# SwiGLU's down projection in seven block products for twelve of 22 hidden tiles

## The chip, the cores and the metric

The kernel runs on one core of one Trainium2 chip. Five engines work side by side, each through its own instructions in order: TensorE (PE, with weight loads shown apart as PEld), VectorE (DVE), ScalarE (ACT), GpSimd (POOL) and SyncE (SP). DMA transfers are issued by SP (plain ones) and by POOL (those that add to their destination). The metric is the device time of one execution in microseconds, as the median of several runs; lower is better.

## The reference

One step of a decoder layer for 512 prompt tokens and 64 sample tokens, 576 columns together: a mixer, a cross attention and a SwiGLU, each with RMS norms. The change lies in the SwiGLU:

```python
u = _rms(x) * g_pre_ffn
f = (jax.nn.silu(u @ w_gate) * (u @ w_up)) @ w_down
x = x + _rms(f) * g_post_ffn
```

The model width is 1024 (8 tiles of 128), the hidden width 2816 (22 tiles of 128). Everything is float32.

## The kernel before

**Products.** Data lie with features on partitions and the 576 tokens in columns. A float32 product is made of three: each operand is split into a high part, rounded to the type float32r by a copy on ACT, and a low part, the difference, by a subtraction on DVE (`split`, lines 191 to 193; for weights `split_w`, 174 to 189). `gemm` (195 to 204) adds high x high, high x low and low x high into one PSUM bank. Weights come by SP into the buffers "raw" (two) or "rawx" (two), their parts go to "whi" and "wlo" (three each).

**Gate and up.** Hidden tiles 0 to 3 are computed in the ordinary way, in a stretch whose order is written out by hand (`plan`, under `manual_schedule`). From tile 4 on, class `Pair` (line 1645) does two hidden tiles at once, first the gate, then the up projection. It takes the weights of two tiles, halves the 1024 inputs into 2 x 512 and the tokens into 2 x 288 (`E`), and computes the 2 x 2 block product with seven block products for eight: sums and differences of weight blocks are formed on DVE (`sums`, `diffs`), split into parts, and each of the seven factors is multiplied by a prepared block of u (`mul`: 4 k-steps x 3 products of 288 columns). The blocks are added in PSUM and between PSUM and SBUF: `early` (factors 0 and 1), `mid` (2, 3, 4) and `late` (5, 6). `late` runs after the next half's `early`. The low part l1 of the first weight tile has the tag "wacc" (two buffers): ACT writes the negative of the rounded value, then a POOL transfer adds the weight itself from DRAM (`low`, line 1659). `done` puts the activation into `gates(j)` (two sets of four tiles, in turn), multiplies by the up half and splits the product into `hh`, `hl`, the operand of the down projection.

**Down.** `down_chunk` runs over the 8 output tiles and two column ranges of 256 and 320 (`HALVES`). For each it adds the products over the hidden tiles of a chunk: chunk 0 over tiles 0 to 7, chunk 1 over 8 to 15, chunk 2 over 16 to 21. The first chunk's results are copied into `f2` (1800), those of the second are added (1804), those of the last are added together with the sums of squares for the last norm (1859, 1903). `hh` and `hl` lie in the slots s0 and s2, `f2` in slot s4.

**Order.** Behind the hand-ordered stretch, which ends with the `mid` of pair 4's up half, a scheduler fixes each engine's order when the kernel is built: it takes the earliest instruction of the program that its own reckoning says is ready. On the chip each engine keeps that order. The program's order there is: pair 6, chunk 0, pairs 8 to 14, chunk 1, pairs 16 to 20, chunk 2, then a hand-ordered end.

Of the kernel before, what the change touches and what calls it, by code (L numbers as in the profile page):

```python
# [11 lines left out]
F32 = mybir.dt.float32  # L12
F32R = mybir.dt.float32r
# [6 lines left out]
P = 128  # L20
T = 576
# [95 lines left out]
def build(nc, tc, ctx, I, O):  # L117
# [1527 lines left out]
    class Pair:  # L1645

        def __init__(s, j, up, hh, hl):
            s.j, s.up, s.hh, s.hl = j, up, hh, hl
# [71 lines left out]
        def done(s, a, i, ps, more=None):  # L1720
# [12 lines left out]
            k = (s.j + a) % 8  # L1733
            split(s.hh[:, k, E[i]], s.hl[:, k, E[i]], g)
# [25 lines left out]
    def pairs(js, hh, hl, last=None):  # L1760

        for j in js:
            for up in range(2):
                if last and j == 4:
                    continue
                with tc.issue_after((pp[1].ev2 if up else pp[0].ev3).ins) if j == 6 else ExitStack():
                    p = Pair(j, up, hh, hl)
# [5 lines left out]
                last = p  # L1773
        return last
# [22 lines left out]

    def ev_first(n_, j, i, ps, m):
# [9 lines left out]
    for n_ in range(2):  # L1808
        at_(14.0 + n_ / 10, lambda n_: pp.append(Pair(4, n_, *H)), n_)
# [192 lines left out]
def pack(inp):  # L2002
# [38 lines left out]
    out["wdown"] = _units(i["w_down"][0], NFFN)  # L2041
# [46 lines left out]
```

## Time and profile before

| | us |
|---|---|
| median of 3 runs | 1123.84 |
| runs | 1121.85 to 1124.16 |
| span of the profiled execution | 1122.0 |

The span runs from the first to the last instruction; what lies around it isn't in it. In the rows that follow, PE, DVE, ACT and POOL are the engines; "ps_g" and "ps_u" are the PSUM banks of a pair's gate and up half, "ps_dn" those of the down projection, "whi" and "wlo" the parts of weights, "wacc" the low part made by an adding transfer, "gt" the gates, "hh" and "hl" the parts of the hidden tiles. A group of instructions shows, after the names and shapes, its count, its busy time and the mean ns of one, and behind the second bar the idle time of the engine just before it with what ended it. In the timeline the columns are start, duration, engine, line and operation. Records of matmuls overlap: their pace is the distance between starts, not their duration. The list of DMA queues gives packets, MB and the share of 16 engines' time. The page gives KB as 1024 bytes: a 128 x 576 float32 tile has 288.

PE's order in the stage, from the timeline: chunk 0 from about 806.7 us, pairs 8 to 14 from 862.5, chunk 1 with the last block products of pair 14 to about 1005, pairs 16 to 20 to 1066, then chunk 2 and the end.

### The profile page before, as it was taken

How to read it: one execution, taken by the hardware profiler on the slowest of the kernel's cores; microseconds unless marked ns; L12 is line 12 of the kernel's file. 1: busy time of each engine (PE TensorE's matmuls, PEld its weight loads, DVE VectorE, ACT ScalarE, POOL GpSimd, SP SyncE). 2: the span in 40 equal slices, each digit the busy share in tenths (PEclk: the TensorE clock that was granted, in tenths of full speed). 3: DMA queues.
4: the chain of work that ended last, by engine and by line, in shares of the span. 5: the costliest groups of instructions: out<-in, count | busy, mean ns of one | idle time of the engine just before them, and what ended most of it. 6: DMA issues, size and time to landing. Idle time of an engine off the chain costs nothing.

```text
span 1122.0 us, 21140 instructions
## 1 busy us (share of the span) xinstructions
PE 1101.1 (98%) x8427; PEld 1051.6 (94%) x8427; DVE 708.8 (63%) x1395; ACT 595.4 (53%) x1076; POOL 219.3 (20%) x305
## 2 busy tenths in 40 slices
PE   9999999999999999999999999999999999999997
PEld 8999889898998999999988889999999999999997
DVE  6796874457786675668654555767623665446655
ACT  6877533355553365656444455635434675236644
POOL 1333544322122121110144301101001110011000
PEclk9999999999999999999999999999999999999999
DMA  6685565535574447863467855643625775257442
GB/s 213 158 164 129 131 175 158 162 86 141 147 203 107 126 145 266 271 241 109 155 236 281 282 181 174 234 145 92 172 82 126 170 162 141 75 126 172 118 140 85
DMA packets 57127, 181.82 MB, mean 162 GB/s; under 512 B 6300, under 2 KB 10524, under 8 KB 56516
## 3 DMA queue, kind: packets, MB, share of 16 engines
q1 hardware_dynamic: 41444, 137.47, 37.9%
q0 software_dynamic: 15296, 42.47, 18.4%
q8 instruction: 66, 1.08, 0.4%
q10 hardware_dynamic: 288, 0.52, 0.1%
q14 instruction: 33, 0.27, 0.1%
HBM read 158.21 MB, written 22.22 MB: 161 GB/s over the span
## 4 chain that ended last, share of the span: by engine, by line
PE 81%; DMA 6%; DVE 4%; issue 4%; ACT 4%; SPq 0%; POOL 0%; DVEq 0%; ACTq 0%; POOLq 0%
PE ps_in L201 5%; PE ps_in L203 5%; PE ps_in L202 5%; PE ps_dn L201 4%; PE ps_dn L203 4%; PE ps_dn L202 4%; PE ps_u L1717 2%; PE ps_u L1716 2%; PE ps_u L1715 2%; PE ps_g L1715 2%; PE ps_o L201 2%; PE ps_g L1716 2%; PE ps_g L1717 2%; PE ps_o L203 2%; PE ps_o L202 2%
## 5 line engine op out<-in xcount | busy, mean ns | idle before, releaser
L181 ACT CAST whi<-raw 128x1024 fp32r<-128x1024 f32 x110 | 114.7, 1045 | 104.9 <-PE ps_dn L202 20.0
L201 PE MATMUL ps_in<-uh,whi 128*128 128x320 f32 (+1 forms) x544 | 165.9, 305 | 0.0
L203 PE MATMUL ps_in<-uh,wlo 128*128 128x320 f32 (+1 forms) x544 | 163.2, 300 | 0.0
L202 PE MATMUL ps_in<-ul,whi 128*128 128x320 f32 (+1 forms) x544 | 162.7, 299 | 0.0
L188 DVE TENSOR_TENSOR wlo<-raw,whi 128x1024 fp32r<-128x1024 f32 (+1 forms) x102 | 102.0, 1000 | 76.0 <-ACT whi L181 75.6
L201 PEld LDWEIGHTS ps_in<-uh,whi 128*128 128x128 f32 x544 | 103.5, 190 | 2.6 <-issue 1.2
L203 PEld LDWEIGHTS ps_in<-uh,wlo 128*128 128x128 f32 x544 | 103.4, 190 | 1.6 <-issue 1.3
L202 PEld LDWEIGHTS ps_in<-ul,whi 128*128 128x128 f32 x544 | 103.5, 190 | 0.7
L201 PE MATMUL ps_dn<-hh,whi 128*128 128x320 f32 (+1 forms) x280 | 82.7, 298 | 0.0
L203 PE MATMUL ps_dn<-hh,wlo 128*128 128x320 f32 (+1 forms) x280 | 81.9, 294 | 0.6 <-DVE wlo L188 0.6
L202 PE MATMUL ps_dn<-hl,whi 128*128 128x320 f32 (+1 forms) x280 | 82.2, 294 | 0.0
L203 PEld LDWEIGHTS ps_dn<-hh,wlo 128*128 128x128 f32 x280 | 52.8, 189 | 0.8 <-DVE wlo L188 0.8
L202 PEld LDWEIGHTS ps_dn<-hl,whi 128*128 128x128 f32 x280 | 52.8, 188 | 0.0
L201 PEld LDWEIGHTS ps_dn<-hh,whi 128*128 128x128 f32 x280 | 52.3, 188 | 0.3 <-ACT hh L192 0.3
L186 POOL DMA_DIRECT2D wlo<-win x32 | 28.3, 885 | 94.5 <-ACT wlo L185 84.1
L1715 PE MATMUL ps_g<-b,whi 128*128 128x288 f32 x144 | 42.6, 296 | 0.8 <-ACT cc L1751 0.6
L1716 PE MATMUL ps_u<-b,whi 128*128 128x288 f32 x144 | 42.5, 295 | 0.0
L1716 PE MATMUL ps_g<-b,whi 128*128 128x288 f32 x144 | 42.5, 295 | 0.0
L1715 PE MATMUL ps_u<-b,whi 128*128 128x288 f32 x144 | 42.5, 295 | 0.0
L201 PE MATMUL ps_o<-mixm_h,whi 128*128 128x256 f32 (+1 forms) x128 | 38.0, 297 | 1.6 <-ACT whi L181 1.6
L201 PE MATMUL ps_xo<-qh,whi 128*128 128x288 f32 x128 | 38.0, 302 | 1.0 <-ACT f_xo L1407 1.0
L201 PE MATMUL ps_xq<-u2h,whi 128*128 128x320 f32 (+1 forms) x128 | 38.2, 303 | 0.0
(731 smaller groups left out, 3650.3 us busy)
## 6 DMA issues: line engine op xcount, KB each, us to landing
raw<-win SPq DMA_DIRECT2D x35, 512.0 KB, 3.8
raw<-wout SPq DMA_DIRECT2D x17, 512.0 KB, 4.2
kva<-kc SPq DMA_DIRECT2D x16, 512.0 KB, 6.5
kva<-vc SPq DMA_DIRECT2D x16, 512.0 KB, 6.3
raw<-wdown SPq DMA_DIRECT2D x16, 512.0 KB, 3.5
raw<-wxq SPq DMA_DIRECT2D x13, 512.0 KB, 3.7
raw<-wgate SPq DMA_DIRECT2D x13, 512.0 KB, 3.6
raw<-wup SPq DMA_DIRECT2D x13, 512.0 KB, 4.8
```

The source lines that it names most:

```text
L181: A.copy(hi[:, :n], raw[:, :n])
L186: G.dma_start(lo[:, a:b], src[:, a:b], accum_op=ALU.add)
L188: e.tensor_tensor(lo[:, a:b], raw[:, a:b], hi[:, a:b].bitcast(F32), op=ALU.subtract)
L201: mm(ps, wh, ah, start=i == 0, stop=False)
L202: mm(ps, wh, al, start=False, stop=False)
L203: m = mm(ps, wl, ah, start=False, stop=i == len(tiles) - 1)
L1715: mm(ps, wh, b[0][:, k, :], start=start and k == 0, stop=False, skip_group_check=True)
L1716: mm(ps, wh, b[1][:, k, :], start=False, stop=False, skip_group_check=True)
L1717: m = mm(ps, wl, b[0][:, k, :], start=False, stop=k == 3, skip_group_check=True)
```

## The change

Chunk 0 now covers hidden tiles 0 to 3 alone, and comes right behind the hand-ordered stretch. Its results go through two small buffers ("ssq") to a DRAM tile `f2_d`, one transfer on SP for each output tile.

The hidden tiles 4 to 9 and 10 to 15 are taken in two sets. A `Down` makes two output tiles from the three pairs of a set as a 2 x 2 block product with seven block products: 7 x 3 k-steps x 3 products of 288 columns. There are four for each set, alternating between the two groups of PSUM banks. Its weights come as two loads of 128 x 768, are added and subtracted on DVE, and are split into f1, f2, f3 (768 columns, tags "whi" and "wlo") and f4 (384 columns twice, in a buffer of the tag "wacc"). `early`, `mid`, `late` are as in `Pair`; `begin` is the order for the first of a set, around the last pair's `late`. `keep` copies PSUM to the result rows on ACT, `plus` adds PSUM to them on DVE, and `store` sends each row by POOL, with an addition in DRAM, into `f2_d`. Row buffers: the first and third Down use "ssq" tiles, the second and fourth a free half of `gt`.

The operands are formed as the pairs finish: `place`, called by `done`, makes four differences on DVE and seven splits (before, four splits) into a tile of 16 x 288 for each pair, which lies in slot s4, s0 or s2 in turn. So `f2` can't lie in s4 meanwhile: it is loaded from `f2_d` by SP after pair 18, in one transfer of 2304 KB. Pairs 16 to 20 and the last chunk are as before. On the host the rows of `w_down` are put in the order of the sets.

The core of the diff:

```diff
+        def place(s, a, i):
+
+            op, ((g11, g12), (g21, g22)) = s.dst(s.j), gates(s.j)
+
+            def put(m, g):
+                split(op[:, m, :], op[:, 7 + m, :], g)
+
+            if (a, i) != (0, 1):
+                put(a + a * i, (g11, g21, g22)[a + a * i])
+                return
+            minus(g11, g12, g11)
+            minus(g12, g22, g12)
+            minus(g22, g22, g11)
+            put(4, g22)
+            put(3, g11)
+            put(5, g12)
+            minus(g21, g21, g22)
+            put(6, g21)
...
+    class Down:
+
+        def __init__(s, c, n_):
+            s.c, s.j = c, 2 * n_
+            s.r1 = wp.tile([P, 1024], F32, name="raw", tag="raw", bufs=2)[:, :768]
+            s.r2 = fp.tile([P, 1024], F32, name="rawx", tag="rawx", bufs=2)[:, :768]
+            for a, r in enumerate((s.r1, s.r2)):
+                S.dma_start(r, I["wdown"][s.j + a, :, 768 * c - 256:768 * c + 512])
+            if n_ % 2:
+                g4 = gates(6 * c + 2)
+                s.st = [[g4[a][i] for i in range(2)] for a in range(2)]
+                s.rows = [gt[:, 4 * ((3 * c + 1) % 2) + 2 * a:4 * ((3 * c + 1) % 2) + 2 * a + 2, :].rearrange("p i t -> p (i t)") for a in range(2)]
+            else:
+                s.rows = [ph.tile([P, 640], F32, name="fst", tag="ssq", bufs=2)[:, :T] for _ in range(2)]
+                s.st = [[r[:, c_] for c_ in E] for r in s.rows]
...
+        def prepare(s):
+            s.f1 = s.parts()
+            split(*s.f1, s.r1)
+            sw_ = sw[:, :768]
+            V.tensor_tensor(sw_[:, DB], s.r2[:, DA], s.r2[:, DB], op=ALU.add)
+            minus(sw_[:, DA], sw_[:, DB], s.r1[:, DA])
+            s.f2 = s.parts()
+            split(*s.f2, sw_)
+            minus(s.r2[:, DA], s.r1[:, DA], s.r2[:, DA])
+            minus(s.r1[:, DB], s.r1[:, DB], sw_[:, DA])
+            s.f3 = s.parts()
+            split(*s.f3, s.r2)
+            t_ = fp.tile([P, 1024], F32R, name="wacc", tag="wacc", bufs=2)
+            s.f4 = t_[:, DA], t_[:, DB]
+            split(*s.f4, s.r1[:, DB])
...
+        def mul(s, ps, w, m, ks=(0, 1, 2), start=True, stop=True):
+
+            fh, fl = (s.f1, s.f2, s.f3, s.f4)[w // 2]
+            for k in ks:
+                c = slice((3 * (w % 2) + k) * P, (3 * (w % 2) + k + 1) * P)
+                op = operand(6 * s.c - 2 + 2 * k)
+                bh, bl = op[:, m, :], op[:, 7 + m, :]
+                mm(ps, fh[:, c], bh, start=start and k == 0, stop=False, skip_group_check=True)
+                mm(ps, fh[:, c], bl, start=False, stop=False, skip_group_check=True)
+                mm(ps, fl[:, c], bh, start=False, stop=stop and k == ks[-1], skip_group_check=True)
...
+        def begin(s, last):
+
+            s.x, y, s.z = s.bank(), s.bank(), s.bank()
+            s.mul(s.x, 0, 0)
+            s.keep(0, 0, s.x)
+            s.mul(y, 1, 1, (0, 1), stop=False)
+            last.late()
+            s.mul(s.z, 3, 3, (0, 1), stop=False)
+            s.mul(s.x, 2, 4, (0, 1), False, False)
+            s.mul(y, 1, 1, (2,))
+            s.plus(0, 0, y)
+            s.mul(s.x, 2, 4, (2,), False)
+            s.keep(0, 1, s.x)
+            s.mul(s.z, 3, 3, (2,))
+            s.end()
...
+        def early(s):
+            s.x, y = s.bank(), s.bank()
+            s.mul(s.x, 0, 0)
+            s.keep(0, 0, s.x)
+            s.mul(y, 1, 1)
+            s.plus(0, 0, y)
+
+        def mid(s):
+            s.mul(s.x, 2, 4, start=False)
+            s.keep(0, 1, s.x)
+            s.z = s.bank()
+            s.mul(s.z, 3, 3)
+            s.end()
+
+        def end(s):
+            s.mul(s.x, 4, 5, start=False)
+            s.keep(1, 1, s.x)
+            s.plus(1, 1, s.z)
+
+        def late(s):
+            s.mul(s.x, 5, 6, start=False)
+            s.keep(1, 0, s.x)
+            s.store(1)
+            s.mul(s.z, 6, 2, start=False)
+            s.plus(0, 1, s.z)
+            s.store(0)
+
+        def store(s, a):
+            G.dma_start(f2_d[:, s.j + a, :], s.rows[a], accum_op=ALU.add)
+
+    def down_blocks(c, last):
+
+        for n_ in range(4):
+            d = Down(c, n_)
+            d.prepare()
+            if n_ == 0:
+                d.begin(last)
+            else:
+                d.early()
+                last.late()
+                d.mid()
+            last = d
         return last
...
     def ev_first(n_, j, i, ps, m):
         t0, n = HALVES[i]
-        A.copy(f2[:, j, t0:t0 + n], ps)
-
-    def ev_add(n_, j, i, ps, m):
-        t0, n = HALVES[i]
-        V.tensor_tensor(f2[:, j, t0:t0 + n], f2[:, j, t0:t0 + n], ps, op=ALU.add)
+        if j not in firsts:
+            firsts[j] = ph.tile([P, 640], F32, name="fst", tag="ssq", bufs=2)
+        A.copy(firsts[j][:, t0:t0 + n], ps)
+        if i == 0:
+            S.dma_start(f2_d[:, j, :], firsts[j][:, :T])
...
+    w_of = lambda j: weights(("d", j), I["wdown"][j, :, 0:512], 512, cut=512)
+    down_chunk(0, 4, [(j, i) for j in range(8) for i in (1, 0)], pp[1], w_of, ev_first)
+    last = down_blocks(1, pairs((6, 8), operand))
+    last = down_blocks(2, pairs((10, 12, 14), operand, last))
+    hh, hl = SL0("hh2"), SL(2, "hl2", F32R)
+    last = pairs((16, 18), (hh, hl), last)
     f2 = SL(4, "f_ffn")
-
-    for c, (js, ev) in enumerate((((4, 6), ev_first), ((8, 10, 12, 14), ev_add))):
-        if c:
-            hh, hl = SL0("hh%d" % c), SL(2, "hl%d" % c, F32R)
-        last = pairs(js, hh, hl, None if c else pp[1])
-        w_of = lambda j: weights(("d", j, c), I["wdown"][j, :, 1024 * c:1024 * c + 1024], cut=1024)
-        down_chunk(c, 8, [(j, i) for j in range(8) for i in (1, 0)], last, w_of, ev)
-
-    hh, hl = SL0("hh2"), SL(2, "hl2", F32R)
-    last = pairs((16, 18, 20), hh, hl)
+    S.dma_start(f2, f2_d)
+    last = pairs((20,), (hh, hl), last)
```

More of the change, by code (lines that the diff above doesn't have):

```diff
@@ L1758, in late, with operand, pairs @@
             s.done(0, 1, s.z, s.c2)
-    def pairs(js, hh, hl, last=None):
+    operands = {}
+    def operand(j):
+        if j not in operands:
+            make = ((lambda n, d, w: SL(4, n, d, w)), (lambda n, d, w: big0.tile(list(w), d, name=n, tag="s0", bufs=1)),
+                    (lambda n, d, w: SL(2, n, d, w)))[(j - 4) // 2 % 3]
+            operands[j] = make("hop%d" % j, F32R, (P, 16, 288))
+        return operands[j]
+    def pairs(js, dst, last=None):
         for j in js:
             for up in range(2):
-                if last and j == 4:
-                    continue
                 with tc.issue_after((pp[1].ev2 if up else pp[0].ev3).ins) if j == 6 else ExitStack():
-                    p = Pair(j, up, hh, hl)
+                    p = Pair(j, up, dst)
                     p.prepare()
@@ L1773, in pairs, with parts, bank, keep @@
                 last = p
+        return last
+    f2_d = dr.tile([P, KT, T], F32, name="f2_d")
+    DA, DB = slice(0, 384), slice(384, 768)
+    class Down:
[12 more added lines that the diff above has]
+                s.st = [[r[:, c_] for c_ in E] for r in s.rows]
+        def parts(s):
+            return [wp.tile([P, 1024], F32R, name=k, tag=k, bufs=3)[:, :768] for k in ("whi", "wlo")]
+        def prepare(s):
[13 more added lines that the diff above has]
+            split(*s.f4, s.r1[:, DB])
+        def bank(s):
+            return (MP if s.j % 4 else GP)("ps_dn")[:, :288]
+        def mul(s, ps, w, m, ks=(0, 1, 2), start=True, stop=True):
[7 more added lines that the diff above has]
+                mm(ps, fl[:, c], bh, start=False, stop=stop and k == ks[-1], skip_group_check=True)
+        def keep(s, a, i, ps):
+            A.copy(s.st[a][i], ps)
+        def plus(s, a, i, ps):
+            V.tensor_tensor(s.st[a][i], s.st[a][i], ps, op=ALU.add)
+        def begin(s, last):
[37 more added lines that the diff above has]
+            G.dma_start(f2_d[:, s.j + a, :], s.rows[a], accum_op=ALU.add)
```

17 lines of the change are left out of this document (11 added, 6 removed).

## The prediction

> **What bounds the kernel now.** I read the page's head first, then the windows over the stages that the change touches, then PE's waits, and last the rows that price each added operation.
>
> ```profile
> span 1122.0 us, 21140 instructions
> PE 1101.1 (98%) x8427; PEld 1051.6 (94%) x8427; DVE 708.8 (63%) x1395; ACT 595.4 (53%) x1076; POOL 219.3 (20%) x305
> ...
> PE 81%; DMA 6%; DVE 4%; issue 4%; ACT 4%; SPq 0%; POOL 0%; DVEq 0%; ACTq 0%; POOLq 0%
> ```
>
> PE is busy for 98% of the span and carries 81% of the chain that ended last, so a product taken away is worth its pitch, unless PE then waits. The next view is the windows: columns are the stretch, its length, then busy time (instructions) of PE, its weight loads, DVE, ACT and POOL, the granted clock, the DMA share and GB/s. The first row is the old first down chunk (all products over hidden tiles 0 to 7), the second two halves of a gate/up pair, the third the old second chunk. The last three serve further down.
>
> ```profile
> 806.70:862.50 55.80, 55.80 (x422) 55.80 (x421) 18.25 (x24) 19.17 (x33) 2.55 (x3) 1.00 0.43 109
> 899.90:922.10 22.20, 22.20 (x170) 22.20 (x169) 15.47 (x29) 15.79 (x26) 3.35 (x5) 1.00 0.76 166
> 947.50:1005.00 57.50, 56.89 (x429) 56.69 (x428) 24.86 (x40) 14.51 (x19) 2.55 (x3) 1.00 0.41 106
> 355.00:360.00 5.00, 2.97 (x22) 1.65 (x20) 4.54 (x7) 3.50 (x8) 2.20 (x3) 0.87 0.68 166
> 360.00:364.00 4.00, 4.00 (x26) 4.00 (x27) 2.94 (x9) 1.14 (x3) 0.00 (x0) 0.74 0.52 121
> 792.00:796.00 4.00, 2.70 (x21) 2.46 (x20) 3.67 (x8) 3.50 (x7) 0.85 (x1) 1.00 0.90 197
> ```
>
> PE stands nowhere in the stages of the change but at three places; its waits from 740 us on (line that waits, for whom, total, times, longest):
>
> ```profile
> PE ps_u L1717 <- DMA wacc<-wup: 1.3, 1, 1.3
> ...
> PE ps_g L1715 <- ACT cc L1751: 0.6, 1, 0.6
> PE ps_dn L203 <- DVE wlo L188: 0.6, 1, 0.6
> ```
>
> So the stage is a solid train of products, and the question is only how many leave it and what new holes come in.
>
> **Products removed.** One half of a pair, seven blocks of 4 x 3 = 84 products of 288 columns, repeats at equal distance in the chain of waits, and the chunk's products (256 and 320 columns in turn) can be paced in the timeline:
>
> ```profile
> 909.71 0.27 PE ps_g L1717 x2
> ...
> 931.93 0.27 PE ps_g L1717 x2
> ```
> ```profile
> 837.04 0.31 PE L201 MATMUL ps_dn<-hh,whi 128*128 128x320 f32 x1
> ...
> 849.79 0.31 PE L201 MATMUL ps_dn<-hh,whi 128*128 128x320 f32 x1
> ```
>
> (931.93 - 909.71) / 168 = 132.3 ns for 288 columns; from 837.04 to 849.79 lie two output tiles' turns, 96 products, so 12.75 / 96 = 132.8 ns on average. Before, chunks 0 and 1 take 2 x 8 x 2 x 8 x 3 = 768 products, 102.0 us. After, the first chunk covers four hidden tiles, 8 x 2 x 4 x 3 = 192 products, 25.5 us; a Down has 7 blocks x 3 k-steps x 3 = 63 products, 8.33 us, and eight of them take 504 products, 66.7 us. Removed: 102.0 - 92.2 = **9.8 us**. The last chunk (tiles 16 to 21) and all gate and up products stay.
>
> **Holes of before that go.** The 1.3 us wait was pair 6's up half standing for its adding transfer, right behind the hand-ordered stretch. Now chunk 0, 25.5 us with nothing for that transfer to wait on, lies between; that wait goes. So does the 0.6 us of the old second chunk (ps_dn for wlo), since the chunk is gone. The 0.6 us at L1751, inside a pair, I leave. **-1.9 us.**
>
> **Operands formed per pair, and the blocks' weights.** The rows, with mean ns before the second bar:
>
> ```profile
> L193 DVE TENSOR_TENSOR hl<-gt,hh 128x288 fp32r<-128x288 f32 x29 | 13.1, 456 | 12.9 <-ACT hh L192 12.9
> L192 ACT CAST hh<-gt 128x288 fp32r<-128x288 f32 x29 | 12.1, 425 | 8.9 <-DVE gt L1732 8.9
> L1672 DVE TENSOR_TENSOR sw<-rawx 128x512 f32<-128x512 f32 x13 | 8.9, 688 | 0.1
> L1740 ACT COPY cc<-ps_g 128x288 f32<-128x288 f32 x7 | 2.8, 399 | 2.0 <-PE ps_g L1717 2.0
> L188 DVE TENSOR_TENSOR wlo<-rawx,whi 128x768 fp32r<-128x768 f32 x1 | 0.9, 948 | 0.0
> L181 ACT CAST whi<-rawx 128x768 fp32r<-128x768 f32 x1 | 0.8, 834 | 0.7 <-PE ps_g L1716 0.7
> ```
>
> place() makes seven splits where there were four, and four differences: per pair +3 x 0.425 = 1.3 us of ACT, +7 x 0.456 = 3.2 us of DVE. A pair's 22.2 us then hold 15.5 + 3.2 = 18.7 us of DVE and 17.1 of ACT: under PE's time. A Down costs DVE three lows of 768 columns (2.84), five operations on 384 columns (between 456 and 688 ns, I take 550: 2.75) and three additions from PSUM (1.37), 7.0 us; ACT three casts (2.50), one of 384 (0.5) and four copies (1.6), 4.6 us; both against PE's 8.33. So I cost them at nothing: PE's own products cover them. Without that cover the extra DVE work would be 6 pairs x 3.2 = 19 us (a rival below).
>
> **The start of each block set (begin).** Here the chain is short of cover. The last up half's late ends with block 6; from there the k = 2 operand of block 4 needs addition, product, three differences, cast and low part. The trace has the old chain of addition, product, cast, low part in two engines:
>
> ```profile
> 953.75 0.46 DVE L1730 TENSOR_TENSOR ct<-ps_u,cc 128x288 f32<-128x288 f32 x1 [4.45 <-ACT cc L1751]
> 954.24 0.46 DVE L1732 TENSOR_TENSOR gt<-gt,ct 128x288 f32<-128x288 f32 x1
> ...
> 955.20 0.46 DVE L193 TENSOR_TENSOR hl<-gt,hh 128x288 fp32r<-128x288 f32 x1 [0.50 <-ACT hh L192]
> ```
>
> 953.75 to 955.66 is 1.91 us. Three dependent differences add up to 3 x 0.49 (the step from the first row to the second): 3.4 us. begin puts 6 + 6 + 3 = 15 products there, 1.98 us. The gap is 1.4 us, and DVE may be within a 948 ns low part when the chain starts; I take 1.7 us, twice **+3.4 us**. Bounds: nothing, where other products are pulled forward, and 2 x 2.4 us, a whole low part in front.
>
> **From blocks back to pairs.** A Down's fourth factor f4 takes the tag "wacc" with two buffers, which the next pair's l1 needs for its adding transfer. The third Down's buffer comes free with block 6 in its late, which stands between early and mid of the fourth Down. From there: ACT writes the negative, POOL issues, the transfer adds. Once in the trace that chain was bare, at the 1.3 us wait:
>
> ```profile
> 788.88 1.06 ACT L1664 ACTIVATE wacc<-raw 128x1024 fp32r<-128x1024 f32 x1 [2.05 <-DMA raw<-wup]
> ```
> ```profile
> 790.25 0.86 POOL L1665 DMA_DIRECT2D wacc<-wup  x1 [7.78 <-ACT wacc L1664]
> ```
> ```profile
> DMA to landing us min/median/max: 5.0/5.6/7.8
> ```
>
> From issue to landing lie 5.6 us at the median, so 1.4 + 5.6 = 7.0 us from the buffer's release. PE has the fourth Down's mid, 27 products, and its late, 18, plus the four products of the pair's first two blocks that need no low part: 49 x 132.3 ns = 6.5 us, if late is pulled ahead of the pair's early. That leaves 0.5 us at the median and 2.7 at the slowest landing; I take 1.0, twice **+2.0 us**. The up half's l1 gets the fourth Down's buffer at 6.5 us and has the gate's 56 remaining products, 7.4 us, as cover: nothing. Bounds: 0, and for the pulled order not taken 7.0 - 27 x 0.1323 = 3.5 us, twice 7.0.
>
> **Result rows and adding transfers.** Each Down sends two rows of 288 KB by POOL, added in DRAM; its row buffers are used again two Downs later, so the first copy (ACT, keep) of the third and fourth Down waits for the landing, with ACT's later casts behind it, and block 2 behind the copy (same PSUM bank). No row shows an addition into DRAM; the nearest are the additions into SBUF:
>
> ```profile
> wlo<-wgate POOLq DMA_DIRECT2D x7, 256.0 KB, 4.8
> ```
> ```profile
> q1 hardware_dynamic: 7073, 24.96, 29.5%
> q0 software_dynamic: 4032, 11.01, 24.2%
> ```
>
> After block 6 the addition takes 0.6 us, the transfer about 5 (between 256 KB at 4.8 and 512 KB at 5.6), the copy 0.4: 6.0 us. Cover, from the same moment: the new Down's early (18), the other's block 4 (9) and late (18), and block 3 (9), 54 products, 7.1 us, if all of it is pulled forward; 27 products, 3.6 us, if none beyond the first two is. Stall between 0 and 2.4 us; four places; I take 0.5 each, nearer to the first, as PE's train of pairs shows such interleaving without holes: **+2.0 us** (bounds 0 and 9.6). By the Trainium skill, "DMA: Bandwidth & Descriptors", Anatomy of one DMA, a transfer costs about 2.0 us plus its bytes over 436 GB/s, here 2.7 us by my estimate, and this term would be 0; the same section warns that a write into HBM is confirmed slowest, which speaks against the change. The trace disagrees with the figure: 256 KB took 4.8 us.
>
> Load on the engines of DMA: 8 first rows and the final return add 4.7 MB at q1's rate (24.96 MB in 29.5% of 280 us: 302 GB/s), 15.6 us; the 16 additions 4.7 MB at q0's 162 GB/s, 29 us. Over the 280 us from 800 to 1080 that is 16% more share; the chunk's rows above show 0.41 and the pairs' 0.76. SP's first-row stores stand in its queue behind ACT's copies, but weights are fetched two buffers ahead there. The return of f2 on SP (2304 KB, 7.8 us at that rate) stands ahead of pair 20's weights and is itself needed only in the last chunk. Cost: nothing, hidden by pairs 18 and 20; without that cover 7.8 us once.
>
> **Sum.** -9.8 - 1.9 + 3.4 + 2.0 + 2.0 = **-4.3 us**. The profiled execution's span, 1122.0, becomes 1117.7. The median of the runs is 1123.84, 1.84 us above that span; so I forecast 1119.5 us.
>
> **Rivals.**
>
> *All holes filled.* The order written by the scheduler pulls later products forward wherever one waits, as it does between the halves of pairs, where PE shows no hole in 22.20 us. Then only -9.8 - 1.9 and at most 1 us of begin stay: 1113.1. Against: in begin the next Down's first factor needs a cast buffer that the first Down still holds, so little can be pulled.
>
> *Nothing gained.* At the two returns to pairs the order is kept as written, 3.5 us each, and begin takes its upper bound, 4.8: -9.8 - 1.9 + 4.8 + 7.0 + 2.0 = +2.1, so 1125.9 at worst and 1123.4 with one of the two returns. For it: the wait at 790 shows that a landing later than reckoned in the order costs PE directly.
>
> *Slower: the row buffers.* If an addition into DRAM lands after the slowest 7.8 us seen, instead of about 5, the keep comes at 0.6 + 7.8 + 0.4 = 8.8 us, against 3.6 us of sure cover: 5.2 us at four places, 21 us in place of 2, so 1138; with all of the 7.1 us, 1.7 us each, and the total stays at 1124. It decides from where a place costs (9.8 + 1.9 - 3.4 - 2.0) / 4 = 1.6 us. A long hole costs more: after PE's 2.0 us of idleness in 355 to 360 the granted clock fell to 0.87 and 0.74, 0.13 x 5 + 0.26 x 4 = 1.7 us lost, while the 1.3 us hole in 792 to 796 left it at 1.00. With that, four holes of 3 us would give 1119.5 - 2 + 4 x 4.7 = 1136. By the Trainium skill, "TensorE: Matmul & The Clock Gate", What's actually happening, the gate closes only after an idle window of about 3.4 us; here it fell after 2.0.
>
> *DVE becomes the bound.* 18.7 of 22.2 us speaks against; if the additions could not overlap, 19 us more, 1138.5.
>
> **How the numbers follow.** Forecast 0.42 (1116 to 1122), all filled 0.22, nothing gained 0.19, row buffers 0.13, DVE 0.04. A difference of 0.2%, 2.2 us, is about what the measurement of this kernel can tell from none: faster is below 1121.6. Faster: 0.22 + 0.9 x 0.42 = 0.60. Same: 0.04 of the forecast and 0.16 of "nothing gained", 0.20; slower the rest, 0.20. The range runs from all filled, 1112.5, to 1130, which takes in returns and begin at their upper bounds with two of the four rows held for 2.4 us, and leaves out most of the last two cases.
>
> **What would show it.** Right: fewer products by 72, DVE about 18.7 us in a pair's 22.2, holes of 1 to 2 us before block 4's k = 2 at the two begins and for the gate's wacc at the two returns, no hole within pairs. Wrong: PE waiting behind ACT copies that wait for f2_d's transfers, a clock below 1.00 there, or products of pairs spaced by DVE; no wait of PE for ps_dn operands at all would make the first rival right.

## The result and the profile after

| | before | after |
|---|---|---|
| median (us) | 1124.0 (4 runs, 1121.85 to 1125.87) | 1152.56 (4 runs, 1149.21 to 1158.25) |
| ratio to before, 95% interval | | 1.0252 [1.0218, 1.0287] |
| span of the profiled execution | 1122.0 | 1156.5 |

The change made the kernel 28.6 us slower; 1119.5 had been forecast, 1130 was the upper end of the range. The head of the page of after:

```profile
span 1156.5 us, 21317 instructions
...
PE 1107.1 (96%) x8355; PEld 1052.0 (91%) x8355; DVE 754.5 (65%) x1501; ACT 621.7 (54%) x1150; POOL 234.2 (20%) x321
...
q0 software_dynamic: 17600, 47.19, 20.0%
...
PE 71%; DMA 12%; issue 6%; ACT 5%; DVE 5%; POOL 0%; SPq 0%; DVEq 0%; ACTq 0%; POOLq 0%
```

PE has 72 instructions fewer (8427 - 8355), which is 768 - 192 - 504: the products left as reckoned. In the chain that ended last PE's share fell from 81% to 71%, DMA's doubled from 6% to 12%.

The profiled execution of after ran 34.5 us longer than that of before, more than the medians differ. To leave out what happens ahead of the change I measure one stretch in every kernel: from the first product of pair 4's gate (764.8 us in the trace of before, 773.7 in that of after) to the end of the span. The windows view of that stretch, first of before, then of after (columns: stretch, length, busy time and instructions of PE, PEld, DVE, ACT, POOL, granted clock, DMA share, GB/s):

```profile
764.80:1122.00 357.20, 348.05 (x2619) 345.86 (x2617) 195.14 (x340) 182.62 (x310) 27.89 (x33) 1.00 0.52 130
```
```profile
773.70:1156.50 382.80, 349.52 (x2547) 342.90 (x2545) 240.92 (x446) 209.14 (x384) 42.55 (x50) 0.98 0.57 146
```

The stretch grew by 25.6 us. PE's idle time in it rose from 357.20 - 348.05 = 9.2 to 382.80 - 349.52 = 33.3 us, 24.1 more; and PE's busy time rose by 1.5 although 72 products, 9.5 us, are gone, so it is 11 us more than the remaining products took at the old pace. Of these 11 us a slower clock makes 5.8 (worked out below). Another part lies in how busy time is counted: a product's record lasts 0.29 us where the pace is 0.13, so each new hole adds what is left of a record, and e7 below, whose granted clock in this stretch is 1.00, still has 342.94 - 338.5 = 4.4 us too many. Nearly everything is new waits, then, and what comes with them. The waits of PE in after, from 740 us on (who waits for whom: total, times, longest):

```profile
PE ps_g L1717 <- DMA wacc<-wgate: 12.3, 2, 6.3
PE ps_dn L1854 <- ACT gt L1859: 2.9, 2, 1.5
PE ps_dn L1854 <- ACT fst L1859: 2.8, 4, 0.8
PE ps_u L1715 <- ACT whi L192: 2.3, 2, 1.2
PE ps_dn L1854 <- ACT whi L192: 2.1, 3, 0.8
PE ps_dn L1856 <- DVE wlo L193: 1.6, 2, 0.8
PE ps_u L1717 <- DMA wacc<-wup: 1.5, 1, 1.5
...
PE ps_u L1715 <- ACT cc L1773: 0.7, 1, 0.7
```

The first row is the two returns from blocks to pairs: PE stands 6 us each time for the low part that the adding transfer makes. Rows two and three are the copies of a Down's results into row buffers (`keep`). In the view of line 1859 ACT itself stands 10.4 us ahead of four of these copies until an earlier row has landed; the two longest waits for fst, 0.8 us each, aren't of that kind, since they stay when no row is stored (e3 below). Rows five and six are operands at the start of each block set.

The first return in detail. POOL's timeline, then the DMA view of 904 to 920 us (issues: KB each, median us to landing):

```profile
906.60 1.76 POOL L1908 DMA_DIRECT2D f_d<-fst  x2 [0.22 <-issue]
907.71 1.55 POOL L1665 DMA_DIRECT2D wacc<-wgate  x1
```
```profile
q0 software_dynamic: 743, 1.72, 65.7%
q1 hardware_dynamic: 414, 1.52, 27.4%
...
f_d<-fst POOLq DMA_DIRECT2D x2, 288.0 KB, 6.2
f_d<-gt POOLq DMA_DIRECT2D x2, 288.0 KB, 9.6
wacc<-wgate POOLq DMA_DIRECT2D x1, 512.0 KB, 10.1
raw<-wgate SPq DMA_DIRECT2D x1, 512.0 KB, 7.9
```

The transfer that PE will wait for is issued at 907.71, in the midst of two rows of the third Down; it lands 10.1 us later, at 917.8, where before the median was 5.6. The queue of adding transfers alone takes 65.7% of all DMA engines here. The plain weight load beside them is late too, 7.9 us. What PE does meanwhile, in windows:

```profile
908.00:912.00 4.00, 3.52 (x27) 3.29 (x25) 3.54 (x8) 2.33 (x4) 1.33 (x3) 1.00 1.08 152
912.00:916.00 4.00, 0.00 (x0) 0.00 (x0) 0.43 (x2) 1.11 (x2) 3.48 (x4) 0.95 1.04 228
916.00:918.00 2.00, 0.17 (x1) 0.17 (x2) 0.00 (x0) 0.00 (x0) 0.00 (x0) 0.50 1.06 291
918.00:922.00 4.00, 4.00 (x17) 4.00 (x18) 0.00 (x0) 0.40 (x1) 0.00 (x0) 0.50 1.10 238
```

The DMA share is above 1.0 from 908 to 922, so the engines of DMA have no time left, and DVE and ACT have next to nothing to do from 912 on, so no compute engine is the bound here. PE's work ends near 911.4; and when it resumes, the granted clock is 0.50.

### The profile page after: what moved, and what is told of

Its sections match the earlier page's. It is cut to its first block, busy times and chain, and to the rows that moved or that the text cites. A ratio compares the mean times of both kernels' runs of the same rounds, so it can differ in the third digit from the quotient of the medians.

```text
span 1156.5 us, 21317 instructions
## 1 busy us (share of the span) xinstructions
PE 1107.1 (96%) x8355; PEld 1052.0 (91%) x8355; DVE 754.5 (65%) x1501; ACT 621.7 (54%) x1150; POOL 234.2 (20%) x321
## 4 chain that ended last, share of the span: by engine, by line
PE 71%; DMA 12%; issue 6%; ACT 5%; DVE 5%; POOL 0%; SPq 0%; DVEq 0%; ACTq 0%; POOLq 0%
PE ps_in L201 5%; PE ps_in L203 5%; PE ps_in L202 5%; PE ps_o L201 2%; PE ps_u L1715 2%; PE ps_o L203 2%; PE ps_u L1717 2%; PE ps_o L202 2%; PE ps_u L1716 2%; PE ps_g L1717 2%; PE ps_g L1715 2%; PE ps_g L1716 2%; PE ps_v L774 2%; DMA wacc<-wgate 2%; PE ps_v L773 2%
## 5 line engine op out<-in xcount | busy, mean ns | idle before, releaser
L181 ACT CAST whi<-raw 128x1024 fp32r<-128x1024 f32 (+1 forms) x102 | 102.9, 1011 | 80.0 <-PE ps_in L202 19.5
L188 DVE TENSOR_TENSOR wlo<-raw,whi 128x512 fp32r<-128x512 f32 (+1 forms) x94 | 87.9, 935 | 59.3 <-ACT whi L181 58.7
L1854 PE MATMUL ps_dn<-hop,whi 128*128 128x288 f32 x144 | 43.9, 309 | 7.9 <-ACT gt L1859 2.9
L1856 PE MATMUL ps_dn<-hop,wlo 128*128 128x288 f32 x144 | 42.1, 303 | 1.6 <-DVE wlo L193 1.6
L1855 PE MATMUL ps_dn<-hop,whi 128*128 128x288 f32 x144 | 43.0, 301 | 0.0
L202 PE MATMUL ps_o<-mixm_l,whi 128*128 128x256 f32 (+1 forms) x128 | 38.5, 301 | 0.0
L774 PE MATMUL ps_v<-wlo,uh 128*128 128x256 f32 x128 | 37.5, 297 | 0.6 <-DMA wlo<-wv 0.6
L203 PE MATMUL ps_o<-mixm_h,wlo 128*128 128x256 f32 (+1 forms) x128 | 38.1, 301 | 0.0
```

What stands on the lines that cost most here:

```text
L181: A.copy(hi[:, :n], raw[:, :n])
L188: e.tensor_tensor(lo[:, a:b], raw[:, a:b], hi[:, a:b].bitcast(F32), op=ALU.subtract)
L202: mm(ps, wh, al, start=False, stop=False)
L203: m = mm(ps, wl, ah, start=False, stop=i == len(tiles) - 1)
L774: m = mm(o, ah, lo[:, j:j + 256], start=False, stop=k == KT - 1, skip_group_check=True)
L1854: mm(ps, fh[:, c], bh, start=start and k == 0, stop=False, skip_group_check=True)
```

## The experiments

The stretch and PE's idle time below come from the windows view of the same stretch in each kernel's trace; idle is its length minus PE's busy time. Runs of the kernel before on the same chips had medians of 1127.17 (e1 to e4), 1126.07 (b0, e5 to e7) and 1126.36 us (e8 to e11).

| run | edit | median us | ratio [95%] | stretch us | PE idle us |
|---|---|---|---|---|---|
| before | | 1124.0 | | 357.2 | 9.2 |
| b0_before | before, once more | 1130.62 (1 run) | | 355.9 | 8.1 |
| after | | 1152.56 | 1.0252 [1.0218, 1.0287] | 382.8 | 33.3 |
| e1_own_f4 | f4 in a place of its own | 1156.42 | 1.0266 [1.0246, 1.0286] | 384.3 | 32.5 |
| e2_sp_stores | rows written plainly | 1145.59 | 1.0167 [1.0133, 1.0201] | 372.4 | 25.3 |
| e3_no_stores | rows not stored | 1144.54 | 1.0158 [1.0133, 1.0183] | 372.8 | 26.7 |
| e4_own_nostores | e1 and e3 | 1135.32 | 1.0062 [1.0035, 1.009] | 364.8 | 21.4 |
| e5_own_sp | e1 and e2 | 1136.95 | 1.0092 [1.0063, 1.0122] | 364.7 | 20.8 |
| e6_dve_lows | returns without adding transfers | 1145.42 | 1.0174 [1.0149, 1.0199] | 375.8 | 26.2 |
| e7_dve_sp | e6 and e2 | 1130.11 | 1.0043 [1.0018, 1.0069] | 359.6 | 16.7 |
| e8_rows | e6, more row buffers | 1137.03 | 1.0108 [1.0067, 1.015] | 372.1 | 24.8 |
| e9_rows_pieces | e8, return of the sum in pieces | 1132.44 | 1.0063 [1.0045, 1.0081] | 362.3 | 17.2 |
| e10_all | e9, pair 6 and the starts | 1129.01 | 1.0035 [1.001, 1.0061] | 361.3 | 16.8 |
| e11_begin_sp | e7, pair 6 and the starts | 1126.95 | 1.0007 [0.9986, 1.0029] | 357.0 | 13.2 |

**The kernel before, once more (b0_before).** No edit.

> The kernel before, profiled beside the others. Every kernel with the change so far reached the last hand-ordered stretch 4 to 9 us later than the kernel before did in its trace, in code that the change does not touch. If that is the chip, this trace is late by 4 us or more too (span about 1126, stretch at 768 to 770 us); if it is the change, it reaches it at 765 us.

This execution's stretch begins at 772.9 us and lasts 355.9. The 8.9 us by which the trace of after was late ahead of pair 4 belong to the execution, then, not to the change, and two executions of before differ by 1.3 us in the stretch. Differences of a microsecond between stretches are not read further.

**One suspect at a time (e1, e3) and both (e4).** My theory after the result: the fourth factor f4 holds the buffer "wacc" that the next pair needs. The rival: the additions in DRAM crowd the DMA. e1_own_f4 puts f4 into free columns of the tiles u3h and u3l:

```diff
-            t_ = fp.tile([P, 1024], F32R, name="wacc", tag="wacc", bufs=2)
-            s.f4 = t_[:, DA], t_[:, DB]
-            split(*s.f4, s.r1[:, DB])
+            c4 = slice(288 + P * (s.j // 2 % 2), 416 + P * (s.j // 2 % 2))
+            s.f4 = u3h[:, 0:3, c4], u3l[:, 0:3, c4]
+            split(*s.f4, K3(s.r1[:, DB]))
...
```

> f4 lies in free columns of u3h and u3l, so the next pair's l1 need not wait for block 6 of the third Down. Theory A (buffer): the two waits of PE for wacc<-wgate, 6.3 and 6.0 us in the changed kernel, fall to under 1 us in sum, the clock stays at 1.00 around the returns, the stage gains 12 us of waits and up to 7 us of half clock: about 1134 us. Theory B (queue): the transfer is slow because additions into DRAM stand ahead of it on POOL's queue; it lands 8 us or later after its issue again and PE waits at least 3 us at each return: about 1143 us.

e3_no_stores drops the 16 adding transfers, so the output lacks the contribution of hidden tiles 4 to 15:

```diff
-            G.dma_start(f2_d[:, s.j + a, :], s.rows[a], accum_op=ALU.add)
+            pass
```

> The Downs' result rows are not sent at all (12 hidden tiles are left out of the result); f4 still shares wacc. Theory A: waits for wacc at the returns 5 us or more each. Theory B: 1 to 2 us each. Both: no wait behind ACT fst or gt, 5.7 us less than the changed kernel.

e4_own_nostores has both edits and leaves out the same sum.

> f4 in its own columns and no rows sent (12 hidden tiles are left out of the result). Both theories: no wait for wacc at the returns and none behind fst or gt; what is left is the begin, about 2 us each, so the stage is 9.8 us of products shorter than before and some 5 us of holes longer: about 1120 us. If it is above 1126, a cause is missing.

e1 gained nothing, and fits neither expectation: the waits on wacc<-wgate are gone, as the theory said, but the time didn't fall to 1134 us, and the granted clock in the stretch is 0.97. Other waits stand in their place (first PE's, then ACT's, then one row of the DMA view of 880 to 1030 us):

```profile
PE ps_dn L1855 <- ACT whi L192: 5.8, 5, 3.2
PE ps_g L1715 <- ACT whi L1669: 5.7, 3, 3.4
PE ps_u L1715 <- DVE ct L1730: 4.6, 1, 4.6
PE ps_u L1715 <- ACT whi L1669: 3.2, 1, 3.2
```
```profile
ACT wacc L1664 <- DMA raw<-wup: 17.4, 6, 6.0
ACT wacc L1664 <- DMA raw<-wgate: 16.1, 7, 5.3
```
```profile
raw<-wgate SPq DMA_DIRECT2D x5, 512.0 KB, 7.8
```

PE now stands for casts on ACT, and ACT, which works in order, stands at L1664 for weights that SP fetched, up to 5.3 us for a gate's and 6.0 us for an up half's. The gate's take 7.8 us from issue to landing. Without the additions, in e4, the same row reads:

```profile
raw<-wgate SPq DMA_DIRECT2D x5, 512.0 KB, 4.1
```

For the up half the two runs don't differ in that way (4.8 us with the additions, 5.7 without). e3 shows what is left at the returns with no row stored:

```profile
PE ps_g L1717 <- DMA wacc<-wgate: 5.5, 2, 3.0
```

That is again neither theory's number (5 us or more each, or 1 to 2). Its two transfers land after 7.9 and 7.4 us, against 10.1 and 9.8 in after. So of the 12.3 us at the returns 5.5 are there without any addition, and 6.8 come with them. In e1, where the buffer is free, the transfer for the first return is issued 124.5 us behind the start of the stretch, against 134.0 in after, and lands after 6.8 us.

With the additions in, freeing the buffer moves the stretch from 382.8 to 384.3; with them out, from 372.8 to 364.8. Taking out the additions is worth 10.0 us with the buffer shared and 19.5 with it free. So neither theory stands alone: the buffer decides when the return starts, the additions make the weights due at that moment late, and with only the buffer freed the lateness shows up at the next load. By the Trainium skill, "Trainium Kernel Development and Optimization", Key Constraints, transfers issued by SP, ACT and POOL all run on the same 16 DMA engines and interleave; the trace agrees, with SP's weights at 7.8 us beside POOL's additions and 4.1 without.

e4 missed its own forecast: about 1120 us were expected, and above 1126 a cause was said to be missing; it took 1135.32. One such cause stands in its trace. ACT waits for the next pair's weights ahead of a `keep`, which PE then waits 1.4 us for although no row is stored:

```profile
899.76 1.06 ACT L1664 ACTIVATE wacc<-raw 128x1024 fp32r<-128x1024 f32 x1 [4.37 <-DMA raw<-wup]
```

The copy starts behind it, at 900.73. Its list of PE's waits has two of these (2.6 us in sum), 2.9 us at casts of weights in the pairs, and the starts; none of the other waits is longer than 1.4 us.

**Stores, or additions? (e2, e5).** e2_sp_stores writes the same rows plainly by SP into a DRAM tile of their own; the sum over the sets is left out, so the output lacks the same contribution. e5_own_sp has e1's edit as well.

```diff
-            G.dma_start(f2_d[:, s.j + a, :], s.rows[a], accum_op=ALU.add)
+            S.dma_start(f3_d[:, 8 * (s.c - 1) + s.j + a, :], s.rows[a])
...
```

> Result rows go by plain transfers on SP into a DRAM tile of their own, so the running result is not added up; f4 still shares wacc. Theory A: PE's waits for wacc at the returns stay at 5 us or more each. Theory B: wacc lands in 5 to 7 us after its issue and the two waits fall to 1 to 2 us each: about 1140 us. The keep waits (ACT fst and gt, 5.7 us in sum) shrink if the addition is what makes a row late, and stay if it is the reuse of two buffers.

> f4 in its own columns and rows sent plainly by SP (the running result is not added up). If the additions in DRAM, not the rows as such, are what the stores cost, this equals the kernel without stores and with own columns: stage 7.6 us longer than the kernel before's, about 1135 us. If rows as such cost, it stands 5 us or more above that.

A plain row costs next to nothing, as e5 expected: 372.4 us of stretch against 372.8 without stores, and 364.7 against 364.8, with medians 1.1 and 1.6 us higher. e2's waits at the returns, 3.1 and 3.6 us, lie again between the two theories; its waits for fst and gt fall from 5.7 to 1.7 us, as when no row is stored (e3). It is the added row on POOL's queue that costs, not the writing as such. The page of e3, beside that of after above, prices it; in between lie just these 16 rows:

```profile
span 1143.2 us, 21273 instructions
...
q0 software_dynamic: 15296, 42.47, 17.5%
```

20.0% of 16 x 1156.5 us are 3701 us of engine time, 17.5% of 16 x 1143.2 are 3201: 500 us for 2304 packets, 0.22 us a packet, or 2 us of all 16 engines for one row. The other pair, e1 (19.8% of 16 x 1152.8) less e4 (17.8% of 16 x 1134.5), gives 421 us, 0.18 us a packet. Plainly written, the same packets stand in q1 and take 38.7% of 16 x 1141.5 (e2) less 37.8% of 16 x 1143.2 (e3), 154 us, and by e5 less e4 230 us: 0.07 to 0.10 us a packet. Adding takes two to three times the engine time of writing.

e2 and e5 change two things at once, the adding and the queue (SP's for POOL's). For the engine time the trace of before tells them apart: from 411 to 489 us POOL issues plain transfers alone, and its queue reads

```profile
q0 software_dynamic: 3149, 11.39, 44.0%
```

That is 11.39 MB in 44.0% of 78 us, 332 GB/s, beside SP's 9.79 MB in 36.7%, 342 GB/s. The added rows, 4.72 MB in 421 to 500 us over 16 engines, move at 151 to 179 GB/s. So the engine time is the adding's, not the queue's. What the place in POOL's queue does to the landing isn't settled by this.

**Returns without adding transfers (e6, e7).** If the returns are the place, forming the low parts of pairs 10 and 16 without a transfer should mend them while the sum is kept. e6_dve_lows fetches the weights of the second tile plainly and subtracts on VectorE:

```diff
+            if s.j in (10, 16):
+                s.direct()
+                return
...
+            S.dma_start(s.r2, s.src[s.j + 1])
+            s.high1()
+            s.l1 = fp.tile([P, 1024], F32R, name="wacc", tag="wacc", bufs=2)
+            V.tensor_tensor(s.l1, s.r1, s.h1.bitcast(F32), op=ALU.subtract)
...
+            V.tensor_tensor(s.l3[:, LA], s.r2[:, LB], s.h3[:, LB].bitcast(F32), op=ALU.subtract)
```

> The first pair behind each set of blocks (tiles 10 and 16) forms its low parts on DVE, so no adding transfer stands in the return, whatever POOL's queue holds and whenever the buffer comes free; the row additions stay. If buffer and queue together made the two waits of 6 us, they fall under 2 us each, the half clock there goes, and the time falls by 15 to 20 us to about 1137 us. If row additions hurt in another way (late loads, ACT behind them), it stays above 1148 us.

e7_dve_sp adds e2's edit and, as there, leaves out the sum.

> As the run before, and rows sent plainly by SP (the running result is not added up). Left are the begins, about 3 us each, and the copies behind them: stage 9.8 us of products shorter, 8 to 12 us of holes longer than before's: about 1127 us. Under 1124 us would say that a version which beats the kernel before exists once the sum is formed cheaply.

e6 gains 7.0 us in the stretch against after, and loses the 12.3 us at wacc. The two waits are gone, as expected; the time is not: 1145.42 us, between the 1137 of the theory and the 1148 of the rival. What remains in its list:

```profile
PE ps_dn L1872 <- ACT gt L1877: 5.6, 2, 3.4
PE ps_u L1733 <- DVE ct L1748: 4.6, 1, 4.6
```

The first is a `keep` behind a row whose addition hasn't landed. The second is pair 18's up half, and SP's timeline shows what was issued just ahead of its second weight tile, the 2304-KB return of the sum:

```profile
1031.05 0.33 SPq L2005 DMA_DIRECT2D f_ffn<-f_d  x1
1031.49 0.37 SPq L1655 DMA_DIRECT2D rawx<-wup  x1
```

Without additions (e7) both go, and the stretch is 359.6; the median, 1130.11, is 3 us above what was expected.

**More row buffers, the return in pieces (e8, e9).** e8_rows gives the third Down of a set rows of its own; e9_rows_pieces brings the sum back in eight loads of 288 KB, behind the weights of pairs 18 and 20.

```diff
+            elif n_ == 2:
+                t_ = rb_tile("fst2")
+                q_ = [ph.tile([P, 320], F32, name="fst3", tag="sq", bufs=2)[:, :288] for _ in range(2)]
+                s.rows = [t_, q_]
...
```
```diff
-    S.dma_start(f2, f2_d)
...
+                if j in (18, 20):
+                    for _ in range(2):
+                        with tc.issue_after(p.ld.ins):
+                            q = pieces.pop(0)
+                            S.dma_start(f2[:, q, :], f2_d[:, q, :])
...
```

> e6_dve_lows with one part more: the third Down of a block of four puts its rows into buffers of its own, so that the fourth finds the buffers of the second's two rows long free. Theory (the rows' additions in DRAM hold their buffers until they land, and the late keeps end in a stretch at half clock): the waits of ps_dn for gt (5.6 us in two) go, with up to 3.4 us of clock behind them; the stretch from pair 4 to the end falls from 375.8 to 367-370 us, the ratio to 1.009-1.012. Rival (the additions only crowd the DMA; a keep that needn't wait for them moves the delay to the next weight load): the waits turn up elsewhere, at ACT's raw or at wacc, and the stretch stays at 374-377 us, ratio 1.016-1.018.

> e8_rows with one part more: the 2304-KB return of the running result comes in eight loads of 288 KB behind the weight loads of pairs 18 and 20, not in one ahead of them. Theory (the one large return holds up pair 18's weight load, which ps_u waits 4.6 us for by way of ct): that wait goes, the stretch falls by a further 4-7 us against e8_rows (362-365 us where e8 gives 368), ratio 1.004-1.008. Rival (the weight load is late because of the additions just ahead of it, not because of the return): the wait stays within 1 us of 4.6 and so does the time of e8_rows.

In e8 the waits on gt are gone, but only 3.7 us of the stretch with them, short of the theory's 6 to 9 though past the rival's; the ratio, 1.0108, is the one that the theory gave. PE stands elsewhere, the longest wait in pair 20 and the one on wacc in pair 18:

```profile
PE ps_g L1733 <- ACT cc L1791: 4.8, 3, 2.6
...
PE ps_g L1735 <- DMA wacc<-wgate: 1.3, 1, 1.3
```

In e9 these two groups are 2.0 and 0.4 us. The stretch falls to 362.3 us, within the 362 to 365 expected, though by 9.8 us where 4 to 7 were expected; the medians fall by 4.6. The wait of 4.6 us that the expectation names can't be what went: it is in e8's list no more than in e9's. So the return in one piece cost time, but by way of other waits than the one that e6 showed.

**Pair 6 and the starts (e10, e11).** Both form pair 6's low part on VectorE and change the order at the start of a set: the last late product of the pair before comes after block 1, and the first Down's f4 is formed behind the start. e11_begin_sp is on top of e7 and leaves out the sum.

```diff
-            last.late()
+            last.late5()
             s.mul(s.z, 3, 3, (0, 1), stop=False)
             s.mul(s.x, 2, 4, (0, 1), False, False)
             s.mul(y, 1, 1, (2,))
             s.plus(0, 0, y)
+            last.late6()
...
```

> e9_rows_pieces with two parts more: pair 6 forms its low part on VectorE instead of by an adding transfer, and at the start of each block the last late product of the pair before comes after the block's third product, with the first Down's fourth operand formed behind the start. Theory (the starts cost some 3 us each because their operands come one after another, and pair 6's 1.5 us is the adding transfer): 3-6 us less than e9_rows_pieces, 357-361 us from pair 4 to the end, ratio 0.999-1.004. Rival (VectorE is full for 12 us at a start, so that its work only changes places): the starts keep their 3 us each, and only pair 6's 1.5 us goes: 1-2 us less than e9_rows_pieces.

> e7_dve_sp (rows written plainly, the sum over blocks left out) with pair 6's low part on VectorE and the start reordered as in e10_all. It bounds what the change could give if the sum cost nothing. Theory: the 9.8 us of products are there and what was left of waits (starts, pair 6) goes in part: 353-357 us from pair 4 to the end where e7_dve_sp has 359.6 and the kernel before 355.9-357.2, ratio 0.997-1.001. Rival (a start's VectorE work is the bound): 358-360 us, ratio 1.002-1.004, so no form of this change that was tried beats the kernel before.

e10's stretch is 1.0 us shorter than e9's, the medians differ by 3.4, and pair 6's wait on wacc is gone. By the times alone theory and rival can't be told apart. The start is untouched, as the windows over it show, first in after, then in e10:

```profile
872.00:878.00 6.00, 4.35 (x29) 3.70 (x28) 5.77 (x13) 2.51 (x6) 0.00 (x0) 1.00 0.22 66
878.00:884.00 6.00, 4.71 (x31) 4.03 (x30) 5.58 (x12) 3.71 (x8) 0.00 (x0) 1.00 0.23 70
```
```profile
864.00:870.00 6.00, 4.34 (x30) 3.74 (x28) 5.72 (x13) 2.50 (x6) 0.00 (x0) 1.00 0.24 66
870.00:876.00 6.00, 4.72 (x31) 3.99 (x31) 5.57 (x12) 3.77 (x8) 0.00 (x0) 1.00 0.22 70
```

DVE is busy for 11.3 of these 12 us and PE for 9.1 in both: VectorE, which forms the pair's operands and the Downs' parts at once, has next to no time left there, and another order of products doesn't help. That VectorE is the bound is argued from this; no run took work from it there. As to the start the rival was right: what was gained isn't the start's. e11's stretch, 357.0, and ratio, 1.0007, are the theory's, at its upper end, but its first start waits as long as that of after (2.9 us). By its times e11 can't be told from the kernel before; its stretch stands between the 355.9 and 357.2 of before. The shortest kernel that keeps the sum is e10, still 0.35% slower than before; none that beats the kernel before was found.

## Why the prediction was wrong

The mechanism forecast was "fewer products, small holes". The products went as forecast; the holes were seven times as large in the one place, and the clock behind them was not in the sum.

- **Products, -9.8:** right, by 72 instructions. At 132.5 ns each that is 9.5 us.
- **Old holes, -1.9:** wrong by 1.5. Pair 6 still waits 1.5 us for wacc<-wup, so chunk 0 in between did not help it. The transfer is issued at 819.86 us, 3.5 us behind the gate half's, and lands after 10.4; no row is being added then, and in e1 to e4 it takes 10.1 to 10.9 us too. Why it takes so long was not tried; with the low part on VectorE (e10, e11) the wait is not there. The 0.6 us of the old chunk 1 went.
- **Starts, +3.4:** 2.1 + 1.6 us at whi and wlo, and two of fst's four, 0.83 each: 5.4 us, where 3.4 had been put and 4.8 had been the upper bound. The place was not the k = 2 operand of block 4 but the factors of the second Down, whose products had been pulled ahead, and the later keep. DVE is full there, which the prediction's mean over a pair, 18.7 of 22.2 us, did not show.
- **From blocks to pairs, +2.0:** this is the step that failed. The wait, the buffer and the place were forecast; the landing was not. It took the median landing of 5.6 us, measured where no rows were being added, and gave 7.8 as the worst. At the two returns it landed after 10.1 and 9.8, among rows on the same queue and with the DMA full; and even with no row stored (e3) after 7.9 and 7.4, so that the waits are 3.0 and 2.5 us where 0.5 had been reckoned at the median. PE's cover, from the last product of the third Down's f4 at 905.65 to 911.4, was 5.7 us where 6.5 had been put, a small miss beside that. Measured: 12.3 us of waits, 2.3 more in the up half that follows, and the clock.
- **Row buffers, +2.0:** undersized, not overlooked: 2.9 at gt and some 1.1 at fst, 4 us, within the stated bound of 9.6. The rival that made the row buffers decide had the sign and the landing time (8.6 us at the median for rows in gt, from the DMA view of after, against the 7.8 it took) but not the place.
- **DMA load at nothing:** this is the step behind the two above. The amount was right: the 16 additions were put at 29 us of all DMA engines, and 421 to 500 us over 16 engines are 26 to 31. What failed was spreading it over 280 us as 16% more share: the rows come in the same microseconds as the weights of the next pair, where the share is 1.04 to 1.10.
- **Return of the sum at nothing:** no wait of after shows it; once other waits are mended, bringing it back in pieces saves 4.6 us by the medians and 9.8 by the stretches (e8 to e9).
- **The clock:** named for the rival alone, at 1.7 us for a long hole, and left out of the sum. In after, by the windows view, PE is busy for 4.6 and 4.8 us in the half-clock stretches at the two returns and for 3.4 us in one at the second start. From 919.20 to 921.60 us ten products follow at 240 ns, against 132.5: of 12.9 us 45% is lost, 5.8 us.

```profile
919.20 0.44 PE L1716 MATMUL ps_g<-u3l,whi 128*128 128x288 f32 x1
...
921.60 0.44 PE L1716 MATMUL ps_g<-u3l,whi 128*128 128x288 f32 x1
```

- **Nothing within pairs:** right. Inside a pair, away from the returns and pair 6, PE waits for cc alone, 0.7 us at most; DVE's extra work there is covered.

These terms, -9.5 - 0.4 + 5.4 + 14.6 + 4 + 5.8, give +20 of the 25.6 us by which the stretch grew; the rest is not assigned to a place. Why even e11, without the sum, only breaks even can be read from the same view: 13.2 us of idle time against 9.2, and 343.85 us of busy time where 348.05 - 9.5 = 338.5 would be left at the old pace. In its list of PE's waits the starts have 4.7 us.

What stays open: whether a wacc transfer is late because it stands behind the rows in POOL's queue or because the DMA engines are full; both hold at that moment, and issuing the rows later was not tried. A full share alone doesn't make a landing late: in before it is 0.97 from 899 to 905 us, and the wacc transfer issued at 899.39 lands after 5.9 us.

## What to carry to other kernels

Price a transfer by what is in flight at the moment it is issued, not by a median from a quiet stage or a share averaged over the stage: a block scheme bunches its stores exactly where the next loads are due. A sum kept in DRAM by adding transfers is paid for in DMA time, so before trading a product for it, find its cover at the point where it lands. And removing one wait on a full resource can move it to the next load, as in e1: test the two suspects together as well as singly.

## What the runs showed of the hardware

Adding into DRAM took 0.18 to 0.22 us of engine time for a packet of 2304 bytes, against 0.07 to 0.10 for writing it. A plain 288-KB row by SP landed after 2.1 us at the median in the best case (rows of fst in e11; those of gt took 4.4 there, and in e2 the two took 3.0 and 5.0; chunk 0's plain rows in after took 5.3), an added one in after 5.7 (fst) or 8.8 (gt). By the Trainium skill, "DMA: Bandwidth & Descriptors", Anatomy of one DMA, my estimate was 2.7 us for such a transfer; the plain rows run from 2.1 to 5.3, the added ones are well above it.

```profile
f_d<-fst SPq DMA_DIRECT2D x8, 288.0 KB, 2.1
```

The clock was not lost by the length of a single hole. Its half-speed stretches start and end on a grid: in after they begin at 915.64, 994.14 and 1035.10 us, 23 and 12 steps of 3.413 us apart, and last one or two steps. Cut along that grid, the windows of after pair up, each with the one behind it:

```profile
878.10:881.51 3.41, 2.96 (x19) 2.60 (x19) 3.38 (x8) 1.45 (x4) 0.00 (x0) 1.00 0.41 123
881.51:884.92 3.41, 2.57 (x20) 2.35 (x19) 2.99 (x5) 2.56 (x5) 0.00 (x0) 1.00 0.16 17
990.73:994.14 3.41, 1.77 (x11) 1.24 (x10) 3.36 (x8) 0.86 (x2) 0.00 (x0) 1.00 0.32 99
994.14:997.56 3.42, 3.42 (x17) 3.42 (x15) 2.72 (x7) 1.77 (x4) 0.00 (x0) 0.50 0.15 30
...
898.57:901.98 3.41, 2.01 (x16) 1.77 (x14) 2.14 (x4) 0.86 (x3) 0.00 (x0) 1.00 1.00 268
901.98:905.40 3.42, 3.42 (x26) 3.42 (x27) 1.44 (x3) 2.31 (x5) 0.00 (x0) 1.00 0.47 134
```

In these rows PE busy for 2.01 us or more of a step left the next at full speed; 1.77 us, here two waits of 0.8 us and their edges, halved it. The busy time isn't the bound, though. In e8 a step with 2.21 us is followed by one at half speed, and one with 1.61 us (from 1050.57 us, 13 products) by one at full speed:

```profile
978.89:982.30 3.41, 2.21 (x12) 1.50 (x11) 3.28 (x7) 2.47 (x5) 0.00 (x0) 1.00 0.40 115
982.30:985.71 3.41, 3.41 (x16) 3.41 (x15) 1.86 (x4) 1.07 (x2) 0.00 (x0) 0.50 0.41 120
```

What separates them is the count of products that the row shows for a step (26 and more where PE never stands). Cut along each trace's own grid, from pair 4 to the end of before, after, e1, e6, e8 and e11, every step at full speed with 12 products or fewer is followed by one at half speed, and every one with 13 or more by one at full speed. That is read off six traces, where most products have 288 columns, and no run was made to test it.

By the Trainium skill, "TensorE: Matmul & The Clock Gate", What's actually happening, a free-running window of 3413 ns decides, which the grid bears out; an idle window, as it says, is not needed, since a step with 12 of 26 products suffices. So the same two waits cost 1.5 us more or nothing, by where they fall on the grid.
